# Expert tokens from a DRAM copy by indirect DMA in place of a one-hot gather on TensorE

## Chip, cores and metric

The kernel runs on one core of one Trainium2 chip. The metric is the device time of one launch in microseconds (us), the median of three runs. The profile is of one execution of the same program, taken by the hardware profiler.

## What is computed

Two layers of an encoder over 512 tokens of 1024 features (float32). Each layer has a mixer of two attention groups, a cross-attention into 256 memory tokens, and a mixture of experts. The last part is the one that matters here:

```python
def expert_choice_moe(h, w_router, w_gate, w_up, w_down):
    cap = EC_CAPACITY_FACTOR * S // N_EXPERTS            # 64 tokens for each of 16 experts
    affinity = jax.nn.softmax((h @ w_router).astype(jnp.float32), axis=-1)
    gate, idx = lax.top_k(jnp.swapaxes(affinity, 1, 2), cap)
    x_in = jax.vmap(lambda hb, ib: hb[ib])(h, idx)       # gather: (16, 64, 1024)
    a = jnp.einsum('becd,edf->becf', x_in, w_gate)       # w_gate, w_up: 1024 x 512 for each expert
    u = jnp.einsum('becd,edf->becf', x_in, w_up)
    y = jnp.einsum('becf,efd->becd', jax.nn.silu(a) * u, w_down)   # w_down: 512 x 1024
    y = y * gate[..., None]
    # y is added up at the tokens' places
```

h is the RMS-normalised x; the kernel gathers x itself and applies the gain and the token's inverse root afterwards. Every expert's weights are read once in a layer: 16 x 12 tiles of 512 KB.

## The kernel before

Everything up to the router works on x, which stays in SBUF, token-major in four blocks of 128 tokens. The rest of a layer, the expert stage, goes like this.

*Routing* (lines 912 to 984). `out_block` (865) adds the last residual to a block of x, `features` and `logits` (875, 887) make its router logits, `affinity` (900) the softmax. DVE then finds each expert's 64 best tokens in eight steps of maximum and replacement (967 to 970), makes a mask and its running sum (974, 975), TensorE (PE) turns both to the tokens' side (980), and `pos` (984) holds each token's slot in each expert, or 0. In layer 1 `warm` (961) issues products that nothing reads behind the last four of the eight steps, and in both layers behind the two turns; in layer 0 PE makes the next layer's memory keys meanwhile (956).

*Copies of x.* `xh` and `xl` (938 to 950) are x split in two float32r parts, by ACT and POOL.

*Gather* (1042 to 1067). The experts go in pairs, 64 slots on each half of the partitions, and two pairs make a group. For a group DVE compares `pos` with `iota` to get one-hot matrices `oh` (1046). PE multiplies `xh` and `xl` with them (1058, 1059), four token blocks each, which gives the group's tokens feature-major, 128 features at a time (`fill`, eight times a group). ACT scales them by the gain into `xg` (1062). `up_half` calls the first three fills of a group ahead of its first products and one before each later step of the first pair.

*A pair* (1159 to 1185). PE's program order for a pair: half of the gate products (`up_half`, 16 records on PE), the transposes of the previous pair's hidden layer (`hid_t`, 1104), the other half, the previous pair's down products (1117), the pair's gate values (`gates`, 1080), half of the up products, the previous pair's `scatter` (1131: products with the transposed selection matrix, which DVE adds to x at 1132), `selection` (1073), the other half. A bank of PSUM is evacuated by ACT and DVE as needed; the hidden layer is made by ACT (silu) and DVE.

*Weights.* `use` (986 to 997) lists the 192 tiles of a layer in the order of their use. A ring of tiles in three pools holds them; `EW_A` and `EW_B` are the numbers of two of the pools. Some tiles of the first round go into places that other tiles take up later (`once`, 1001). Loads go out on SP's queue in the order of use; a load waits until PE has used up the tile whose place it takes. The first 17 tiles of layer 0 and 24 of layer 1 (`early`) are loaded before the routing, the rest of the first round during it.

The order within an engine is made by the Tile framework from the program's order and readiness as it models it, so it can differ a little from the program text. The line that fills xg:

```python
nc.scalar.activation(e.xg[:, d, :], pg[:, i * P:i * P + P], AF.Copy, scale=gain(l, G_FFN, d))
```

Of the kernel before, what the change touches and what calls it, by code (L numbers as in the profile page):

```python
# [9 lines left out]
F32 = mybir.dt.float32  # L10
F32R = mybir.dt.float32r
AF = mybir.ActivationFunctionType
ALU = mybir.AluOpType
# [15 lines left out]
EW_B = 8  # L29
# [28 lines left out]
def kernel(ctx: ExitStack, tc: tile.TileContext, a: dict, out: bass.AP):  # L58
# [4 lines left out]
    ps = ctx.enter_context(tc.tile_pool(name="ps", bufs=8, space=PSUM))  # L63

# [9 lines left out]
    # ---------------------------------------------------------------- constants  # L74
# [28 lines left out]
    # ---------------------------------------------------------------- helpers  # L103
# [17 lines left out]
    class Weights:  # L121
        """weight chunks in the order of their use, loaded and split one ahead"""
# [29 lines left out]
    class Norm:  # L152
        """RMS over the features of a token-major tile, from the sums over its two halves"""
# [10 lines left out]
        def rstd(self, b):  # L164
            """mean square + eps -> v, its inverse root -> r"""
# [12 lines left out]
    def softmax_exp(pool, s, n, groups=1, scale=None):  # L178
        """exp of the rows of s (PSUM [P, groups*n]), scaled, less their maximum, and the row sums"""
# [24 lines left out]
    # ================================================================ layers  # L204
    for l in range(L):
# [18 lines left out]
        def gemm_tok(his, los, ks, n, post=()):  # L224
            """all token blocks x n columns; post[chunk, block]: work emitted behind that part"""
# [40 lines left out]
        # ---------------- mixer input projection  # L266
# [23 lines left out]
        def rope_tables():  # L290
            """rope tables with the q / k gains (and the q scale) folded in"""
# [24 lines left out]
        def rope_heads(pt, b, dst, nh, tab):  # L316
            """RMS-norm and rope of nh heads of 64 in PSUM -> dst, [P, nh, 64] each"""
# [59 lines left out]
        # ---------------- attention: units of one 128-query block of one head, heads in pairs  # L377
# [34 lines left out]
        class Group:  # L412
            """one head group's output: RMS norm over its 512 features, its half of w_o, residual"""
# [865 lines left out]
```

## Time and profile before

| | us |
|---|---|
| median of three runs | 1239.08 (1237.15 to 1239.32) |
| span of the profiled execution | 1236.1 |
| time of the profiled execution as a run | not listed apart |
| PE busy | 1196.0 |
| DVE, ACT, POOL busy | 621.5, 513.8, 199.1 |
| weight and other bytes moved | 247.97 MB, 201 GB/s over the span |

The span runs from the first to the last instruction in the profile; a run's time has some 3 us around it. The profile names engines PE (matrix products), PEld (weight loads of PE, beside it), DVE, ACT, POOL and SP; a q behind the name is the engine's instruction or DMA queue. A float32 product stands as two records. "L1098" is line 1098 of the kernel. Busy PE is not PE at its peak, since products are pipelined; idle time of an engine off the path costs nothing.

### The profile page before, as it was taken

The page shows a single profiled execution, that of the slowest core. Times are in us where ns is not written, and L with a number is a line of the kernel's source. Part 1 is how long each engine was busy: PE and PEld are TensorE (multiplying, and loading weights), DVE is VectorE, ACT ScalarE, POOL GpSimd, SP SyncE. Part 2 cuts the span into 40 slices and gives each one's busy share as a digit, 9 for nine tenths or more (in the row PEclk, how much of TensorE's full clock was granted, in tenths as well). Part 3 has the DMA queues.
Part 4 walks back from the last instruction along what each step waited for, and adds up shares of the span by engine and source line. Part 5 has one row for each costly group of instructions (what it writes and reads, how often), then busy time and mean ns, then how long its engine had stood idle before and what let it go on. Part 6 is the DMA issues. An engine that isn't in the chain of part 4 may idle for free.

```text
span 1236.1 us, 17348 instructions
## 1 busy us (share of the span) xinstructions
PE 1196.0 (97%) x6356; PEld 781.5 (63%) x6356; DVE 621.5 (50%) x1389; ACT 513.8 (42%) x1148; POOL 199.1 (16%) x234
## 2 busy tenths in 40 slices
PE   7999999999999999999999899999997999999995
PEld 7977777887773545443399677778864544443432
DVE  4898876556451222222377987755466032322124
ACT  5388766545432212120154886755553211110203
POOL 2533323100030000000124343230004000000002
PEclk9999999999999999999999999999997899999998
DMA  5410011493089999998124000128604599999942
GB/s 192 133 52 18 18 35 35 143 335 136 21 321 360 355 409 400 409 361 340 56 78 153 18 18 18 35 75 312 227 18 184 178 408 356 409 402 409 352 159 85
DMA packets 75621, 247.97 MB, mean 201 GB/s; under 512 B 8208, under 2 KB 18320, under 8 KB 75536
## 3 DMA queue, kind: packets, MB, share of 16 engines
q1 hardware_dynamic: 75104, 246.23, 52.9%
q8 instruction: 50, 0.82, 0.3%
q10 hardware_dynamic: 432, 0.63, 0.2%
q14 instruction: 35, 0.29, 0.1%
HBM read 244.73 MB, written 2.10 MB: 200 GB/s over the span
## 4 chain that ended last, share of the span: by engine, by line
PE 90%; DVE 5%; ACT 2%; issue 1%; POOL 1%; DMA 1%; SPq 0%; POOLq 0%; ACTq 0%; DVEq 0%
PE ps L1098 20%; PE ps L144 11%; PE ps L145 10%; PE ps L146 10%; PE ps L1117 9%; PE ps L1131 5%; PE ps L407 5%; PE ps L393 4%; PE ps L1058 3%; PE ps L1059 3%; DVE smm L181 2%; PE ps L488 1%; PE ps L804 1%; PE ps L847 1%; PE ps L250 1%
## 5 line engine op out<-in xcount | busy, mean ns | idle before, releaser
L1098 PE MATMUL ps<-ew,xg 128*64 128x512 f32 x1024 | 257.2, 602 | 0.0
L114 DVE TENSOR_TENSOR y<-ps,y 128x512 fp32r<-128x512 f32 x32 | 22.1, 692 | 234.0 <-ACT y L113 233.7
L1098 PEld LDWEIGHTS ps<-ew,xg 128*64 128x64 f32 x1024 | 69.0, 136 | 111.0 <-issue 96.7
L1117 PE MATMUL ps<-ew,hT 128*64 128x512 f32 x512 | 120.6, 594 | 0.0
L114 DVE TENSOR_TENSOR wlo<-raw,whi 128x1024 fp32r<-128x1024 f32 (+2 forms) x72 | 82.3, 1146 | 56.8 <-ACT whi L113 55.0
L181 DVE TENSOR_REDUCE smm<-ps 128x1 f32<-128x512 f32 (+1 forms) x144 | 97.7, 682 | 17.6 <-PE ps L488 7.0
L1132 DVE TENSOR_TENSOR x<-ps,x 128x512 f32<-128x512 f32 x128 | 80.0, 684 | 52.0 <-PE ps L1131 52.0
L187 ACT ACTIVATE P<-ps,smm 128x512 f32<-128x512 f32 x128 | 88.8, 697 | 27.9 <-DVE smm L181 22.3
L113 ACT CAST whi<-raw 128x1024 fp32r<-128x1024 f32 (+2 forms) x72 | 70.0, 974 | 65.6 <-PE ps L145 36.8
L196 POOL TENSOR_TENSOR P<-P,smr 128x512 f32<-128x512 f32 x64 | 70.4, 1100 | 155.8 <-DVE smr L194 127.0
L113 ACT CAST y<-ps 128x512 fp32r<-128x512 f32 x32 | 18.8, 587 | 157.8 <-PE ps L1117 138.5
L1117 PEld LDWEIGHTS ps<-ew,hT 128*64 128x64 f32 x512 | 37.6, 137 | 70.8 <-issue 67.5
L393 PE MATMUL ps<-ident,P 128*128 128x128 f32 x512 | 76.7, 273 | 4.0 <-POOL P L196 1.9
L1062 ACT ACTIVATE xg<-ps,gains 128x128 f32<-128x128 f32 x128 | 40.1, 364 | 95.1 <-PE ps L1059 94.9
L144 PE MATMUL ps<-whi,hTh 128*128 128x384 f32 (+2 forms) x224 | 79.0, 353 | 0.2 <-ACT whi L113 0.2
L145 PE MATMUL ps<-whi,hTl 128*128 128x384 f32 (+2 forms) x224 | 78.1, 348 | 0.0
L146 PE MATMUL ps<-wlo,hTh 128*128 128x384 f32 (+2 forms) x224 | 77.8, 350 | 0.0
L393 PEld LDWEIGHTS ps<-ident,P 128*128 128x128 f32 x512 | 62.1, 140 | 24.3 <-issue 3.9
L1131 PE MATMUL ps<-y,sel 128*128 128x512 f32 x256 | 69.1, 408 | 1.5 <-ACT y L113 1.5
L1131 PEld LDWEIGHTS ps<-y,sel 128*128 128x128 f32 x256 | 45.3, 188 | 38.5 <-issue 22.7
L1058 PEld LDWEIGHTS ps<-oh,xh 128*128 128x128 f32 x256 | 48.7, 191 | 32.7 <-issue 30.0
L1058 PE MATMUL ps<-oh,xh 128*128 128x256 f32 x256 | 68.2, 302 | 0.0
(224 smaller groups left out, 2272.6 us busy)
## 6 DMA issues: line engine op xcount, KB each, us to landing
ew<-moe SPq DMA_DIRECT2D x382, 512.0 KB, 8.6
raw<-w_o SPq DMA_DIRECT2D x16, 512.0 KB, 3.2
raw<-w_mem_v SPq DMA_DIRECT2D x8, 512.0 KB, 4.0
raw<-w_mem_q SPq DMA_DIRECT2D x8, 512.0 KB, 4.1
raw<-w_mem_o SPq DMA_DIRECT2D x8, 512.0 KB, 3.6
raw<-w_in_c SPq DMA_DIRECT2D x8, 416.0 KB, 3.7
raw<-w_in_a SPq DMA_DIRECT2D x8, 384.0 KB, 4.7
raw<-w_in_b SPq DMA_DIRECT2D x8, 384.0 KB, 3.8
```

What stands on the lines that cost most here:

```text
L113: i = nc.scalar.copy(dst_hi, src)
L114: nc.vector.tensor_tensor(out=dst_lo, in0=src, in1=dst_hi.bitcast(F32), op=ALU.subtract)
L144: nc.tensor.matmul(o, lh, rh, start=start, stop=False)
L145: nc.tensor.matmul(o, ll, rh, start=False, stop=False)
L146: nc.tensor.matmul(o, lh, rl, start=False, stop=stop)
L181: nc.vector.tensor_reduce(out=m, in_=s.rearrange("p (g n) -> p g n", g=groups), axis=AX.X, op=ALU.max, negate=True)
L187: nc.scalar.activation(p[:, g * n:(g + 1) * n], s[:, g * n:(g + 1) * n], AF.Exp, bias=m[:, g:g + 1], scale=1.0 if scale is None else scale ...
L393: nc.tensor.transpose(pt[:, tb * P:(tb + 1) * P], u.p[:, tb * P:(tb + 1) * P], ident)
L1058: nc.tensor.matmul(pg[:, :256], xh[:, b, d * P:(d + 1) * P], oh[:, b, :], start=b == 0, stop=False)
L1098: nc.tensor.matmul(acc[i * 64:i * 64 + 64, :], e.xg[:, k, i * 64:i * 64 + 64], ch[i][j % 2], start=k == 0, stop=k == 7)
L1117: nc.tensor.matmul(e.py[i * 64:i * 64 + 64, :], e.hT[:, f, i * 64:i * 64 + 64], ch[i][j], start=f == 0, stop=f == 3)
L1131: nc.tensor.matmul(o, sl, e.y[n][i], start=i == 0, stop=i == 1)
```

## The change

In each layer x's blocks are written to a DRAM tensor `xrows` as the router needs them. For each pair, four products of its one-hot matrix with the gate values, to which two columns of token numbers are added, give gates and token numbers together; DVE copies the numbers to integers, and POOL issues an indirect DMA that fetches the 128 rows of 1024 features. PE transposes them (`features_of`), and ACT fills xg with the gain as before. `xh`, `xl` and the gather products are gone. Pairs 0 and 1 are fetched at the start, pair p + 2 in the midst of pair p. The one-hot matrices have two buffers. `EW_B` goes from 8 to 12, and `once` loses its first two places. The `warm` products take x in float32, 256 columns, where they took xh with 512. The last block's output goes into ring tiles where it went into xh's place. Comments and docstrings are removed as well.

```diff
-EW_B = 8
+EW_B = 12
...
+    hbm = ctx.enter_context(tc.tile_pool(name="hbm", bufs=1, space=bass.MemoryType.DRAM))
...
+    ids = const.tile([P, NB], F32, name="ids")
...
+        nc.sync.dma_start(ids, a["ids"])
...
+        xrows = hbm.tile([S, D], F32, name=f"xrows{l}")
...
             if n == 1:
+                nc.scalar.dma_start(xrows[b * P:(b + 1) * P, :], x[:, b, :])
                 ffn_norm.rstd(b)
...
-        affs = mp.tile([P, NB, NE, 2, 2], F32R, name=nm("affs"))
+        affs = mp.tile([P, NB, NE // 2, 10], F32R, name=nm("affs"))
...
-        for b in range(NB):
-            nc.scalar.copy(xh[:, b, :], x[:, b, :])
-            nc.gpsimd.tensor_tensor(out=xl[:, b, :], in0=x[:, b, :], in1=xh[:, b, :].bitcast(F32), op=ALU.subtract)
...
+        for q in range(NE // 2):
+            nc.gpsimd.tensor_copy(affs[:, :, q, 8:10], ids.unsqueeze(2).broadcast_to([P, NB, 2]))
...
-        work = mp.tile([P, 2, S], F32, tag="oh", name=nm("work"), bufs=1)
+        work = mp.tile([P, 2, S], F32, tag="oh", name=nm("work"), bufs=2)
...
-                nc.tensor.matmul(idle, xh[:, 0, 0:P], xh[:, 0, 0:512], start=True, stop=True)
+                nc.tensor.matmul(idle[:, 0:256], x[:, 0, 0:P], x[:, 0, 0:256], start=True, stop=True)
...
-        once = {7: ((mp, "sg", 1), (mp, "sel", 1)), 21: (mp, "xg", 3), 22: (mp, "y", 2), 23: (mp, "y", 2)}
+        once = {22: (mp, "y", 2), 23: (mp, "y", 2)}
...
+        def features_of(e, n):
+            if n == 0:
                 e.xg = mp.tile([P, ND, P], F32, tag="xg", name=nm("xg"), bufs=3)
-
-            def fill(d):
-                pg = bank()
-                for b in range(NB):
-                    nc.tensor.matmul(pg[:, :256], xh[:, b, d * P:(d + 1) * P], oh[:, b, :], start=b == 0, stop=False)
-                    nc.tensor.matmul(pg[:, :256], xl[:, b, d * P:(d + 1) * P], oh[:, b, :], start=False,
-                                     stop=b == NB - 1)
-                for i, e in enumerate(prs):
-                    nc.scalar.activation(e.xg[:, d, :], pg[:, i * P:i * P + P], AF.Copy, scale=gain(l, G_FFN, d))
...
+            pt = bank()
+            for i in range(4):
+                d = n * 4 + i
+                nc.tensor.transpose(pt[:, i * P:(i + 1) * P], e.rows[:, d * P:(d + 1) * P], ident)
+            for i in range(4):
+                d = n * 4 + i
+                nc.scalar.activation(e.xg[:, d, :], pt[:, i * P:(i + 1) * P], AF.Copy, scale=gain(l, G_FFN, d))
...
-        def gates(e):
+        def fetch(e):
             pgt = bank()
             for b in range(NB):
-                nc.tensor.matmul(pgt[:, 0:8], e.oh[:, b, :],
-                                 affs[:, b, 2 * e.p:2 * e.p + 2].rearrange("p e h c -> p (e h c)"),
-                                 start=b == 0, stop=b == NB - 1)
-            e.gt = mp.tile([P, 2], F32, tag="gt", name=nm("gt"), bufs=2)
+                nc.tensor.matmul(pgt[:, 0:10], e.oh[:, b, :], affs[:, b, e.p, :], start=b == 0, stop=b == NB - 1)
+            at_row = mp.tile([P, 1], mybir.dt.int32, tag="row", name=nm("row"), bufs=4)
+            nc.vector.tensor_copy(at_row, pgt[:, 8:9])
+            e.rows = mp.tile([P, D], F32, tag="rows", name=nm("rows"), bufs=2)
+            nc.gpsimd.indirect_dma_start(out=e.rows, out_offset=None, in_=xrows,
+                                         in_offset=bass.IndirectOffsetOnAxis(ap=at_row, axis=0))
+            e.gt = mp.tile([P, 2], F32, tag="gt", name=nm("gt"), bufs=4)
...
+        one_hot(0)
+        for e in prs[:2]:
+            fetch(e)
+        for n in range(2):
+            features_of(prs[0], n)
+        for e in prs:
+            end = e.p == NE // 2 - 1
+            if e.p % 2 == 0 and not end and e.p + 2 < NE // 2:
+                one_hot(e.p // 2 + 1)
+            ag = bank()
+            up_half(e, ag, 0, 0)
+            if prev is not None:
+                hid_t(prev)
+            if not end:
+                features_of(prs[e.p + 1], 0)
+            up_half(e, ag, 0, 1)
...
+            up_half(e, au, 1, 0)
+            if not end:
+                features_of(prs[e.p + 1], 1)
+                if e.p + 2 < NE // 2:
+                    fetch(prs[e.p + 2])
+            if prev is not None and not end:
+                for n in range(2):
+                    scatter(prev, n)
+            if not end:
+                selection(e)
+            up_half(e, au, 1, 1)
```

## Rows read from the trace of the kernel before

**Rows 1.** The page, part 1: busy us, share of the span, instructions.

```profile
PE 1196.0 (97%) x6356; PEld 781.5 (63%) x6356; DVE 621.5 (50%) x1389; ACT 513.8 (42%) x1148; POOL 199.1 (16%) x234
```

**Rows 2.** Stretches: length, busy us of engines (x count), clock, DMA share, GB/s.

```profile
380.00:586.00 206.00, 205.90 (x1000) 93.05 (x1000) 50.27 (x94) 34.23 (x80) 0.00 (x0) 1.00 0.98 383
...
1020.00:1040.00 20.00, 20.00 (x108) 9.26 (x108) 1.09 (x4) 4.89 (x13) 0.00 (x0) 1.00 0.88 326
1040.00:1060.00 20.00, 20.00 (x98) 8.58 (x95) 6.56 (x12) 1.86 (x3) 0.00 (x0) 1.00 1.03 411
```

**Rows 3.** The chain that ended last, layer 1: start us, us, engine and line.

```profile
981.20 3.58 PE ps L1098 x16
...
992.27 0.59 PE ps L1104 x4
...
1043.10 3.86 PE ps L1131 x16
...
1209.31 0.66 PE ps L1104 x4
...
1220.66 1.89 PE ps L1117 x8
```

**Rows 4.** By line, 980 to 1180: busy us, mean ns, idle before, releasers.

```profile
L1098 PEld LDWEIGHTS ps<-ew,xg 128*64 128x64 f32 x412 | 27.2, 136 | 43.6 <-issue 37.1 <-DMA ew<-moe 2.4 <-ACT xg L1062 0.9
```

**Rows 5.** Weight loads of layer 1, then SP's waits (us in total, times, longest).

```profile
L1021 SPq DMA_DIRECT2D ew<-moe x156: 327/328/1177, 970.4 to 1182.0; - x156
...
DMA to landing us min/median/max: 3.6/9.2/11.0
...
SPq L1021 <- PE ps L1098: 94.0, 44, 18.3
```

**Rows 6.** Timeline near 1000 to 1034: start us, us, engine, line, idle before.

```profile
1003.24 0.61 PE L1080 MATMUL ps<-affs,oh 128*128 128x8 f32 x4
...
1003.88 0.15 DVE L1087 COPY g<-ps 64x2 f32<-64x2 f32 x1 [2.63 <-PE ps L1080]
...
1015.09 0.39 PE L1058 MATMUL ps<-oh,xh 128*128 128x256 f32 x1
...
1031.94 2.31 PE L1117 MATMUL ps<-ew,hT 128*64 128x512 f32 x10
```

**Rows 7.** Stretches of 2 us in layer 1, columns as in rows 2.

```profile
944.00:946.00 2.00, 0.01 (x1) 0.00 (x0) 1.88 (x4) 2.00 (x4) 1.85 (x5) 0.65 0.56 185
...
962.00:964.00 2.00, 2.00 (x7) 1.71 (x7) 1.43 (x4) 0.00 (x0) 0.00 (x0) 0.50 0.00 0
...
966.00:968.00 2.00, 2.00 (x14) 1.19 (x13) 0.00 (x0) 1.44 (x5) 0.00 (x0) 1.00 0.03 8
```

**Rows 8.** Timeline, start of the expert stage in layer 0.

```profile
343.73 12.25 PE L847 MATMUL ps<-ew,ew 128*128 128x256 f32 x56
...
358.51 1.44 DVE L1046 TENSOR_TENSOR oh<-pos,iota 128x256 fp32r<-128x256 f32 x4
...
359.12 0.28 PE L1058 MATMUL ps<-oh,xh 128*128 128x256 f32 x1
```

**Rows 9.** Timeline, start of the expert stage in layer 1.

```profile
951.28 1.65 PE L965 MATMUL ps<-xh 128*128 128x512 f32 x3
...
956.45 1.21 DVE L975 TENSOR_TENSOR_SCAN work<-ones,work 16x512 f32<-16x512 f32 x1
...
959.16 0.60 PE L980 MATMUL ps<-ident,work 16*128 16x16 f32 x4
...
962.10 1.43 DVE L1046 TENSOR_TENSOR oh<-pos,iota 128x256 fp32r<-128x256 f32 x4 [0.23 <-PE ps L963]
963.02 0.33 PEld L1058 LDWEIGHTS ps<-oh,xh 128*128 128x128 f32 x1
```

**Rows 10.** Small transfers: KB, median us to landing; then ns of an ACT issue.

```profile
out<-fo SPq DMA_DIRECT2D x4, 512.0 KB, 2.7
...
L1192 ACTq DMA_DIRECT2D lnf<-lnf x1: 334/334/334, 1212.2 to 1212.2; - x1
```

More of the change, by code (lines that the diff above doesn't have):

```diff
@@ L1039, with one_hot @@
         class Experts:
-        def gather(g):
-            oh = mp.tile([P, NB, 256], F32R, tag="oh", name=nm("oh"), bufs=1)
+            pass
+        prs = [Experts() for _ in range(NE // 2)]
+        ohs = {}
+        def one_hot(g):
+            oh = mp.tile([P, NB, 256], F32R, tag="oh", name=nm("oh"), bufs=2)
             for b0, nb in ([(b, 1) for b in range(NB)] if g == 0 else [(0, NB)]):
@@ L1094, in up_half @@
                     ch = [chunk(2 * e.p + i, w * 4 + k // 2) for i in range(2)]
-                while e.fill and len(e.fill) > ND - 3 - k:
-                    e.fill.pop(0)()
                 for i in range(2):
@@ L1134, in scatter @@
                     if b == 0:
-                        e.out = mp.tile([P, NB, D], F32, tag="xh", name=nm("fo"))
-                    nc.gpsimd.tensor_tensor(out=e.out[:, b, ns], in0=x[:, b, ns], in1=lnf[:, ns], op=ALU.mult)
+                        e.out = []
+                    pool, tag, bufs = ring[(len(use) + b - len(ring) - len(once)) % len(ring)]
+                    e.out.append(pool.tile([P, D], F32, tag=tag, name=nm("ew"), bufs=bufs))
+                    nc.gpsimd.tensor_tensor(out=e.out[b][:, ns], in0=x[:, b, ns], in1=lnf[:, ns], op=ALU.mult)
                 elif last:
@@ L1139, in scatter @@
                     last_norm.rstd(b)
-                    final(b, e.out[:, b, :])
+                    final(b, e.out[b])
         def half(b, n):
@@ L1158 @@
         prev = None
-        for g in range(4):
-            for e in gather(g):
-                ag = bank()
-                up_half(e, ag, 0, 0)
-                if prev is not None:
-                    hid_t(prev)
-                up_half(e, ag, 0, 1)
-                if prev is not None:
-                    for n in range(2):
-                        down(prev, n)
-                gates(e)
-                au = bank()
-                up_half(e, au, 1, 0)
-                end = e.p == NE // 2 - 1
-                if prev is not None and not end:
-                    for n in range(2):
-                        scatter(prev, n)
-                if not end:
-                    selection(e)
-                up_half(e, au, 1, 1)
-                if end:
-                    scatter(prev, 0)
-                sg = mp.tile([P, FF], F32, tag="sg", name=nm("sg"), bufs=1)
-                nc.scalar.activation(sg, ag, AF.Silu, scale=e.gt[:, 1:2])
-                nc.vector.scalar_tensor_tensor(out=sg, in0=au, scalar=e.gt[:, 0:1], in1=sg, op0=ALU.mult, op1=ALU.mult)
-                e.hid = sg
-                before, prev = prev, e
+        one_hot(0)
@@ new lines @@
+        for e in prs[:2]:
[13 more added lines that the diff above has]
+            up_half(e, ag, 0, 1)
+            if prev is not None:
+                for n in range(2):
+                    down(prev, n)
+            au = bank()
+            up_half(e, au, 1, 0)
[4 more added lines that the diff above has]
+            if prev is not None and not end:
+                for n in range(2):
+                    scatter(prev, n)
+            if not end:
+                selection(e)
+            up_half(e, au, 1, 1)
+            if end:
+                scatter(prev, 0)
+            sg = mp.tile([P, FF], F32, tag="sg", name=nm("sg"), bufs=1)
+            nc.scalar.activation(sg, ag, AF.Silu, scale=e.gt[:, 1:2])
+            nc.vector.scalar_tensor_tensor(out=sg, in0=au, scalar=e.gt[:, 0:1], in1=sg, op0=ALU.mult, op1=ALU.mult)
+            e.hid = sg
+            before, prev = prev, e
```

21 lines of the change are left out of this document (10 added, 11 removed).

## The prediction, made before the changed kernel was run

> **What bounds the kernel now.** I read the page first, then the busy time by stretch, then TensorE's own timeline, the chain that ended last, the waits on weights, the DMA queue, and the start of the expert stage in both layers. TensorE (PE) is busy 97% of the span [rows 1]. Each expert stage, about 359 to 620 us and 963 to 1236 us, is a stretch in which PE never rests (205.9 of 206 us) while the weight stream runs at 383 GB/s, and at 411 GB/s in its best 20 us [rows 2]. The reader is to see that two resources stand near their limits here, so that taking work from one pays only until the other binds.
>
> Which one binds now is read from three places. The chain that ended last goes through PE pieces almost alone in this stage [rows 3]. PE waited for weights 2.4 us in 200 [rows 4]. And the stream dips to 326 GB/s in a stretch in which PE makes gather products, since a weight tile is loaded only when PE has released one. So PE is the bound and the stream follows it; before the first release SP stands still 18.3 us [rows 5].
>
> **The gather products leave.** In layer 1 a whole group's gather lies between 1015.09 and 1031.94 us on PE, 16.85 us [rows 6]. In it stand two up halves at 3.58 us and one set of four transposes at 0.59 us [rows 3]. What is left, 16.85 - 7.16 - 0.59 = 9.1 us, is the 64 products and their changeovers. Four groups make 36.4 us in a layer. In layer 1 the first group's first two microseconds ran at a granted clock of 0.50 [rows 7], which is 1.0 us more: 37.4 us. All of it lies on the path. The 16 activations that fill xg for a group stay the same in number, so ACT gains nothing.
>
> **The transposes come.** Eight for a pair, in two sets of four like those of the hidden layer: 0.59 us a set [rows 3]. Sets of pairs 1 to 7: 14 x 0.59 = 8.3 us a layer, on the path. Pair 0's belong to the start, below.
>
> **The start of each stage.** Before, the first gather product follows the first of four one-hot blocks; layer 0: blocks from 358.51 to 359.95, product at 359.12 [rows 8]; layer 1: 962.10 to 963.53, PE at 963.02 [rows 9]. Afterwards PE can do nothing useful until x's rows are there. The steps: the last row-number product and its copy on DVE, about 0.65 us after the last block (four gate products started at 1003.24 had DVE start at 1003.88 [rows 6]); the indirect DMA, F; four transposes and the first activation, 1.1 us (0.59, and 0.5 estimated from that same hand-over). No indirect DMA, nor any DMA from POOL, stands in the trace. F is bounded below by the quickest 512 KB transfer, 2.7 us [rows 10], and above by the slowest weight landing, 11.0 us [rows 5]. Below zero is excluded, since nothing can start earlier. In layer 0 the weights are still streaming in at that moment, so I take 7; in layer 1 the queue is idle and I take 5, nearer the quiet row, with something for POOL's issue.
> First up product, layer 0: 359.95 + 0.65 + 7 + 1.1 = 368.7, that is 9.6 us after the old first gather product. Layer 1: 963.53 + 0.65 + 5 + 1.1 = 970.3, 7.3 us after.
>
> The clock: PE lost its full clock within two microseconds of falling idle (0.65 in 944 to 946 us) and worked at 0.50 still at 962 to 964 us [rows 7]. A wait of five microseconds or more will cost it again; it came back within some 3 us of dense work (1.00 at 966 to 968), so half speed costs 1.5 us, in each layer.
>
> Trainium skill, "DMA: Bandwidth & Descriptors", section on the GpSimd path: a DMA takes about 2.0 us plus its bytes over 436 GB/s. For 512 KB that would be 3.2 us; by it the whole sum below would be 5.6 us better. No run here shows it yet.
>
> **The warm-up products in layer 1** change from 512 columns of fp32r to 256 of fp32. An fp32 product of 256 columns takes 12.25/28 = 0.44 us at full clock [rows 8], so 0.88 at half; three make 2.6 us against 1.65 now [rows 9]. They already delay the routing: the mask is ready when the scan starts, 956.45, but PE turns it only at 959.16 [rows 9]. If the clock stays at half, four calls and the later single product make 4.3 us; if the denser products bring the clock up, the 2.7 us of delay could vanish instead. Between -2.7 and +4.3 I take +2, since the clock stayed at 0.50 throughout this pattern before.
>
> **Edits costed at little.** The four writes of x to DRAM go out on ACT's queue: 0.33 us of issue each [rows 10]. Three are hidden under a PE that is full there; the last stands before the copies that the last logits wait for: 0.3 us a layer. If an issue had to wait for a weight transfer ahead of it, ACT would be held for up to that transfer's 9.2 us, in layer 0 alone, where weights load at that moment; I keep that for the range. Their 2.1 MB are 5.1 us of transfers at 411 GB/s, before PE wants weights. The POOL subtractions and ACT casts of x lay beside DVE's top-k steps, which last until 956.45 [rows 9]: nothing gained. The eight index copies on POOL take their place under the same cover. The ids load is one more small DMA on SP at the start, behind work of PE. The tiles: 37 and 38 weights are loaded before PE starts, instead of 35 and 36 (four tiles more, two places of the first round fewer).
>
> **The fetches of later pairs** are issued one pair ahead. Between issue and use PE has a scatter 3.86, two up halves 7.16 and two sets of transposes 1.2: 12.2 us [rows 3]; less 1.7 for the hand-overs, F may be 10.5 without cost. I count nothing; pair 2 has no scatter before it, so some 3.9 us less cover. POOL, which waits for the row numbers, has nothing behind them in its queue until the last norm; DVE's copy of them waits for PE, and behind it stand the gate copies and the scatter's additions, on an engine busy for 50 of 206 us [rows 2].
>
> **Does the weight stream hold?** Before, 156 of a layer's 192 tiles were loaded after the start of layer 1 [rows 5]; with 38 ahead it is 154, and six fetches of the same size; at 0.524 MB over 411 GB/s [rows 2], 1.28 us each, 205 us. From about 972 us they are issued by 1177 and landed by 1186 (9.2 us [rows 5]). The last down products start at 1220.66 before [rows 3], so about 1202 afterwards: 16 us to spare.
>
> **Sum.** Layer 0: -36.4 + 8.3 + 9.6 + 1.5 + 0.3 = -16.7. Layer 1: -37.4 + 8.3 + 7.3 + 1.5 + 2 + 0.3 = -18.0. Together -34.7 on a span of 1236.1: 1201.4. The runs' median stands 3.0 us above that span, the profiled execution having no time of its own in the list: **1204 us**.
>
> **Rivals.**
> *The stream binds.* 221 us for 160 transfers (205 and the 16 to spare) are 380 GB/s; if the fetches, or two queues side by side, push it lower, PE waits at the end of each stage. Speaking for it: it already runs within 7% of its best on average [rows 2], and seven tiles are in flight at a time (9.2 us at 1.28). Against: the dips are PE's own. At 351 GB/s 160 transfers take 239 us, 18 too many in each layer, and nothing is left of the gain; midway, at 365, they take 230, 9 too many: 1222. At the dip's 326 it would be 257 and a loss. Chance 0.20, of which 0.05 at no change.
> The Trainium skill, same page, table of specifications, has about 358 GB/s as the HBM limit of one core: by it 160 transfers would take 234 us, and the time would be 1230. The trace does not agree: 411 GB/s [rows 2].
>
> *The rows come late for every pair.* PE takes its instructions in order; a transpose that waits for rows holds all up products behind it. Place: the first set of transposes of pairs 2 to 7, 12 in all. Price: 12 x (F - 10.5), and 2 x (F - 6) for the starts. It ends slower than before from F = 12.5 us on (24 + 13 = 37); at F = 14 it is 42 + 16 = 58, so 1262 us. For it: weight tiles take up to 11.0 us to land when the queue is full [rows 5], and no row shows what POOL needs to issue such a DMA. Against: a transfer on a queue of its own need not stand behind the seven weight tiles in flight. Chance 0.13.
>
> **Chances.** The forecast, 1193 to 1216 (both F at their ends give -6.6 to +10, the warm-up -4.7 to +2.3), 0.62; the stream 0.20; late rows 0.13; better than 1193, 0.05. What lies within 0.2%, some 2.5 us, a measurement of this kernel can't tell from no change. Faster: 0.62 + 0.15 + 0.05 = 0.82; same 0.05; slower 0.13. The range 1193 to 1232 holds the forecast and most of the first rival.
>
> **What would show it.** Right: the hidden layer's transposes, 31.0 us apart on average now (992.27 to 1209.31 for seven pairs [rows 3]), about 28.3 apart (less 27.3/7, plus 1.2); no gather lines; PE's first up product near 369 and 970 us; no wait of the transposes on the fetch beyond pair 0; the stream near 400 GB/s to the end. Wrong: PE waiting for weights by tens of microseconds late in a stage (first rival), or twelve waits on rows (second), or a first fetch of over 11 us.

## The result and the profile after

The changed kernel takes 1206.05 us (median of 4 runs, 1205.18 to 1207.55), the kernel before 1238.93 us (4 runs, 1237.15 to 1239.32): a ratio of 0.9738 with a 95% interval of 0.9724 to 0.9751. The forecast was 1204 us, faster. The profiled execution has a span of 1203.9 us and took 1205.65 us.

The page of the changed kernel: busy time and share of TensorE, its granted clock in 40 slices, and the chain that ended last, by engine and by line (up products are L1108 now, down products L1127, scatter products L1141, the transposes of fetched rows L1072).

```profile
PE 1146.7 (95%) x5992; PEld 741.2 (62%) x5992; DVE 622.8 (52%) x1405; ACT 500.5 (42%) x1140; POOL 197.6 (16%) x258
...
PEclk9999999999998999999999999999999799999998
...
PE 82%; DMA 7%; DVE 6%; ACT 2%; issue 1%; POOL 0%; SPq 0%; POOLq 0%; DVEq 0%; ACTq 0%
PE ps L1108 17%; PE ps L147 11%; PE ps L148 10%; PE ps L149 10%; PE ps L1127 8%; PE ps L1141 5%; PE ps L410 5%; DMA ew<-moe 4%; PE ps L396 4%; DMA rows<-xrows,row 2%; PE ps L1072 2%; DVE smm L184 2%; PE ps L491 2%; PE ps L807 1%; PE ps L253 1%
```

TensorE is busy for two points less of a shorter span [rows 1]. Two DMA entries stand in the chain, the fetch of the rows (2%) and the weights (4%). The first is the price that was forecast. Of the second some 36 us lie in layer 1, between 1118 and 1163 us, and point to something that was not.

By layer, between the same instructions of both kernels: from the last out-projection addition of layer 0 to the next layer's first transposes 620.27 - 337.55 = 282.7 us before and 607.02 - 337.33 = 269.7 after, so -13.0 (forecast -16.7); the mixer of layer 1 317.7 and 317.4; its expert stage to the end of the span 298.2 and 279.5, so -18.7 (forecast -18.0).

The start of the expert stage of layer 0 after the change, from the timeline (start, duration, engine, line, operation, count, and in brackets the idle time before it with what ended it), and of layer 1 behind the dots:

```profile
359.71 2.57 DVE L1056 TENSOR_TENSOR oh<-pos,iota 128x256 fp32r<-128x256 f32 x5
...
360.80 1.14 PE L1089 MATMUL ps<-affs,oh 128*128 128x10 f32 x8
362.19 0.15 DVE L1091 CAST row<-ps 128x1 int32<-128x1 f32 x1
...
363.21 1.21 POOL L1093 DMA_INDIRECT rows<-xrows,row  x1 [15.94 <-DMA ew<-moe]
...
370.90 1.94 PE L1072 MATMUL ps<-ident,rows 128*128 128x128 f32 x8 [8.97 <-DMA rows<-xrows,row]
...
372.77 4.82 PE L1108 MATMUL ps<-ew,xg 128*64 128x512 f32 x16
...
395.61 0.66 PE L1072 MATMUL ps<-ident,rows 128*128 128x128 f32 x4 [1.49 <-DMA rows<-xrows,row]
...
952.59 1.08 POOL L1093 DMA_INDIRECT rows<-xrows,row  x1 [18.87 <-DVE gt L1100]
...
957.05 1.94 PE L1072 MATMUL ps<-ident,rows 128*128 128x128 f32 x8 [5.62 <-DMA rows<-xrows,row]
...
958.92 5.29 PE L1108 MATMUL ps<-ew,xg 128*64 128x512 f32 x16
```

From POOL's issue to the first transpose the rows take 7.7 us in layer 0, beside a full weight stream, and 4.5 in layer 1, beside an idle one. TensorE stands idle 8.97 and 5.62 us and then starts at half clock: eight transposes take 1.94 us, and the first 16 up records 4.82 and 5.29 where 3.58 is usual [rows 3]. In front of the row number stands a one-hot block that nobody needs yet: the fifth of the five DVE instructions, 1.14 us, is that of the next group. Of the later fetches only pair 2's is waited for, 1.49 us here and 0.41 in layer 1. The clock, in stretches of 4 us (TensorE busy, granted clock, DMA share, GB/s):

```profile
362.00:366.00 4.00, 0.00 (x0) 0.87 1.03 421
366.00:370.00 4.00, 0.00 (x0) 0.50 1.02 413
370.00:374.00 4.00, 3.10 (x12) 0.50 0.54 213
```

TensorE's last product before them ended at 361.9 us; within the first of these stretches the clock fell to the lower of its two levels, 1.2 GHz.

### The profile page after: what moved, and what is told of

It is laid out like the page before. It is cut to its first block, busy times and chain, and to the rows that moved or that the text cites. A ratio compares the mean times of both kernels' runs of the same rounds, so it can differ in the third digit from the quotient of the medians.

```text
span 1203.9 us, 16694 instructions
## 1 busy us (share of the span) xinstructions
PE 1146.7 (95%) x5992; PEld 741.2 (62%) x5992; DVE 622.8 (52%) x1405; ACT 500.5 (42%) x1140; POOL 197.6 (16%) x258
## 4 chain that ended last, share of the span: by engine, by line
PE 82%; DMA 7%; DVE 6%; ACT 2%; issue 1%; POOL 0%; SPq 0%; POOLq 0%; DVEq 0%; ACTq 0%
PE ps L1108 17%; PE ps L147 11%; PE ps L148 10%; PE ps L149 10%; PE ps L1127 8%; PE ps L1141 5%; PE ps L410 5%; DMA ew<-moe 4%; PE ps L396 4%; DMA rows<-xrows,row 2%; PE ps L1072 2%; DVE smm L184 2%; PE ps L491 2%; PE ps L807 1%; PE ps L253 1%
## 5 line engine op out<-in xcount | busy, mean ns | idle before, releaser
L1108 PE MATMUL ps<-ew,xg 128*64 128x512 f32 x1024 | 256.6, 604 | 0.3 <-DMA ew<-moe 0.3
L1108 PEld LDWEIGHTS ps<-ew,xg 128*64 128x64 f32 x1024 | 74.6, 138 | 138.4 <-issue 121.6
L1127 PE MATMUL ps<-ew,hT 128*64 128x512 f32 x512 | 118.5, 594 | 0.2 <-DMA ew<-moe 0.2
L116 ACT CAST y<-ps 128x512 fp32r<-128x512 f32 x32 | 18.7, 585 | 157.0 <-PE ps L1127 154.2
L1127 PEld LDWEIGHTS ps<-ew,hT 128*64 128x64 f32 x512 | 38.0, 137 | 72.9 <-issue 70.0
L1141 PE MATMUL ps<-y,sel 128*128 128x512 f32 x256 | 70.3, 411 | 1.5 <-ACT y L116 1.5
L1093 POOL DMA_INDIRECT rows<-xrows,row x16 | 15.4, 962 | 332.0 <-DVE g L1099 296.5
L399 ACT COPY PT<-ps 128x512 f32<-128x512 f32 x96 | 56.0, 588 | 24.5 <-PE ps L396 24.0
L1141 PEld LDWEIGHTS ps<-y,sel 128*128 128x128 f32 x256 | 45.4, 188 | 31.6 <-issue 17.0
L1075 ACT ACTIVATE xg<-ps,gains 128x128 f32<-128x128 f32 x128 | 36.3, 372 | 67.7 <-PE ps L1072 67.7
```

The costliest lines, as they stand in the source:

```text
L116: i = nc.scalar.copy(dst_hi, src)
L1108: nc.tensor.matmul(acc[i * 64:i * 64 + 64, :], e.xg[:, k, i * 64:i * 64 + 64], ch[i][j % 2], start=k == 0, stop=k == 7)
L1127: nc.tensor.matmul(e.py[i * 64:i * 64 + 64, :], e.hT[:, f, i * 64:i * 64 + 64], ch[i][j], start=f == 0, stop=f == 3)
L1141: nc.tensor.matmul(o, sl, e.y[n][i], start=i == 0, stop=i == 1)
```

## The experiments

Two theories stood at first. **TensorE bounds the stage**: what the change took out of it (about 28 us in a layer) comes off the time, less the wait at the start. **The weight stream bounds it**, or rows are late: then work on TensorE is worth little. All twelve runs, with the kernel before on the same chip beside each:

| run | median us (range) | ratio to the kernel before, 95% interval |
|---|---|---|
| fixed rows at the start | 1191.3 (1190.8 to 1191.7) | 0.9621 (0.9605 to 0.9637) |
| half the weight bytes | 1169.3 (1167.8 to 1169.8) | 0.9440 (0.9424 to 0.9456) |
| before, gathered once | 1189.3 (1188.6 to 1189.3) | 0.9601 (0.9585 to 0.9618) |
| fetched twice | 1276.1 (1274.0 to 1277.2) | 1.0307 (1.0290 to 1.0324) |
| program order | 1185.2 (1185.0 to 1185.6) | 0.9580 (0.9550 to 0.9610) |
| program order, gains on POOL's queue | 1179.8 (1178.5 to 1181.5) | 0.9534 (0.9503 to 0.9564) |
| before, program order | 1214.9 (1211.7 to 1215.7) | 0.9823 (0.9792 to 0.9854) |
| eight tiles | 1204.8 (1203.3 to 1205.5) | 0.9741 (0.9710 to 0.9773) |
| idle products in the wait | 1177.3 (1176.3 to 1179.2) | 0.9519 (0.9502 to 0.9537) |
| and one-hots later | 1176.9 (1175.9 to 1178.1) | 0.9509 (0.9493 to 0.9525) |
| program order, gains, eight tiles | 1188.6 (1187.1 to 1189.0) | 0.9604 (0.9587 to 0.9621) |
| one-hots later, eight tiles | 1183.0 (1181.9 to 1185.8) | 0.9567 (0.9548 to 0.9586) |

**Fixed rows at the start.** Pairs 0 and 1 take their rows from token numbers that are known early; emitted before the top-k steps.

```diff
+        for i in range(2):
+            nc.vector.tensor_copy(at_row, ids[:, i:i + 1])
...
+            nc.gpsimd.indirect_dma_start(out=t, out_offset=None, in_=xrows,
+                                         in_offset=bass.IndirectOffsetOnAxis(ap=at_row, axis=0))
```

> The changed kernel, but pairs 0 and 1 of each layer get fixed token rows, fetched before the routing is known (the output is that of other tokens for these two pairs). Theory (the layer's start waits for the rows, and PE is otherwise the bound): the idle time of 8.97 and 5.62 us ahead of the first transposes goes, and so does what the low clock behind it cost (transposes 1.94 instead of about 1.3 us, the first 16 up products 4.75 and 5.22 instead of 3.58 us, together about 4 us): 1206 - 18.6 = 1187 us, 1184 to 1191. Rival (the weight stream sets the end of the stage, so an earlier start is given back as waits on weights): over 1200 us, with waits of PE on weights of ten us and more where there are 0.5 now.

Measured 1191.3, 14.7 us less than the changed kernel. The waits ahead of pair 0 are gone, and its up products run at full clock (this kernel's timeline):

```profile
362.56 3.65 PE L1119 MATMUL ps<-ew,xg 128*64 128x512 f32 x16
...
945.09 3.65 PE L1119 MATMUL ps<-ew,xg 128*64 128x512 f32 x16
```

So the waits and the half clock at the start are what was supposed. But 4 us of their price did not come off, and the time lies 0.3 us above the theory's range: in layer 0 the first pair's hidden transposes came 11.4 us earlier (382.09 for 393.46) and the last pair's only 7.7 (583.39 for 591.08), with 0.3 us of waits on weights in the records. Something later in the layer gives back; the distances below show where.

**Fetched twice.** Each fetch from pair 2 on is made a second time into the same tile.

```diff
-            nc.gpsimd.indirect_dma_start(out=e.rows, out_offset=None, in_=xrows,
+            for _ in range(2 if e.p > 1 else 1):
+                nc.gpsimd.indirect_dma_start(out=e.rows, out_offset=None, in_=xrows,
```

> The changed kernel, in which each fetch from pair 2 on is issued twice into the same tile; the second waits for the first to land, so the rows come after about 16.5 us instead of 8. Theory (a fetch is hidden as long as it is shorter than the stretch of PE work from its issue to its transposes, which the trace of the changed kernel shows as 7.5 us for pair 2, 11.1 us for pairs 3 to 5 and 14.0 us for pairs 6 and 7): PE waits 9.0, 3 times 5.4 and 2 times 2.5 us in a layer, against 1.49 and 0.41 us now, so about +57 us with both layers: 1263 us, 1245 to 1278, and slower than the kernel before. Rival (the transposes have far more slack than that, since other work runs ahead): within 10 us of 1206 us.

Measured 1276.1, at the top of the theory's range. TensorE's waits on rows in its list of waits (us in all, times, longest):

```profile
PE ps L1072 <- DMA rows<-xrows,row: 62.5, 13, 9.3
```

and three of them in the timeline of layer 0 (pairs 2, 3 and 6):

```profile
401.66 1.12 PE L1072 MATMUL ps<-ident,rows 128*128 128x128 f32 x4 [8.79 <-DMA rows<-xrows,row]
...
436.19 1.12 PE L1072 MATMUL ps<-ident,rows 128*128 128x128 f32 x4 [4.44 <-DMA rows<-xrows,row]
...
537.09 0.73 PE L1072 MATMUL ps<-ident,rows 128*128 128x128 f32 x3 [2.06 <-DMA rows<-xrows,row]
```

Expected were 9.0, 5.4 and 2.5. Of the 70 us the waits make 46.0 (62.5 for 16.5). The rest goes with a lower clock: the same 5992 TensorE instructions are busy 1169.0 us for 1146.7, at a mean granted clock of 0.96 for 0.985, and behind a wait of 4 us a set of transposes takes 1.12 us for 0.66. The rival of late rows was therefore real; the changed kernel is clear of it by 11.1 us of cover against landings of 7 to 9.

**Half the weight bytes.**

```diff
-                nc.sync.dma_start(t, src)
-                parts = [t[:, i * 512:i * 512 + 512] for i in range(2)]
+                nc.sync.dma_start(t[:, 0:512], src[:, 0:512])
+                parts = [t[:, 0:512] for i in range(2)]
```

> The changed kernel with only the first half of each expert weight tile loaded, and used for both halves (wrong weights, the same instructions on PE, half the bytes). Theory (PE bounds the expert stage, its waits on weights are 0.5 us in all): no gain from the weights themselves; only the fetches land sooner beside a thinner stream, which is worth at most the wait of pair 2 (1.49 and 0.41 us) and some 3 us at the start of layer 0 (landing 7.6 us there, 4.3 us in layer 1, where the queues were emptier): 1200 to 1206 us. Rival (the weight stream has become the bound of the stage): under 1190 us.

Measured 1169.3: 36.8 us less, where the first theory had at most 6. Read at face value, the stream is the bound. But TensorE had waited 0.5 us for weights in the changed kernel. What differs shows in the distance of one pair's hidden transposes to the next pair's, which I then read for every kernel (layer 0, us):

| kernel | pairs 0 to 7 |
|---|---|
| before | 33.4, 28.6, 33.4, 27.7, 38.3, 28.9, 26.8 |
| changed | 28.7, 27.0, 27.0, 27.3, 31.0, 30.5, 26.1 |
| fixed rows at the start | 28.5, 26.9, 27.3, 31.0, 31.0, 30.5, 26.1 |
| half the weight bytes | 27.0, 27.0, 27.0, 27.0, 27.0, 26.6, 19.9 |

The changed kernel runs at 27.0 and then loses 4.0, 3.9 and 6.2 us against half the bytes. With fixed rows one pair more is long (31.0 for 27.3): that is what was given back. In the changed kernel's timeline between 503.46 and 534.49 us TensorE is busy for 30.9 of 31.0 us (with some rows left out):

```profile
506.49 5.37 PE L1108 MATMUL ps<-ew,xg 128*64 128x512 f32 x24
511.69 7.04 PE L1127 MATMUL ps<-ew,hT 128*64 128x512 f32 x32
518.56 1.02 PE L1108 MATMUL ps<-ew,xg 128*64 128x512 f32 x2
...
520.37 0.48 PE L1141 MATMUL ps<-y,sel 128*128 128x512 f32 x1
520.78 1.93 PE L1108 MATMUL ps<-ew,xg 128*64 128x512 f32 x6
522.64 0.96 PE L1141 MATMUL ps<-y,sel 128*128 128x512 f32 x3
523.53 1.07 PE L1108 MATMUL ps<-ew,xg 128*64 128x512 f32 x2
524.53 0.96 PE L1141 MATMUL ps<-y,sel 128*128 128x512 f32 x3
525.43 1.93 PE L1108 MATMUL ps<-ew,xg 128*64 128x512 f32 x6
527.29 2.37 PE L1141 MATMUL ps<-y,sel 128*128 128x512 f32 x9
...
529.89 4.51 PE L1108 MATMUL ps<-ew,xg 128*64 128x512 f32 x18
```

and the same pair with half the bytes:

```profile
499.32 3.65 PE L1108 MATMUL ps<-ew,xg 128*64 128x512 f32 x16
502.80 7.04 PE L1127 MATMUL ps<-ew,hT 128*64 128x512 f32 x32
509.67 3.60 PE L1108 MATMUL ps<-ew,xg 128*64 128x512 f32 x16
...
514.06 3.98 PE L1141 MATMUL ps<-y,sel 128*128 128x512 f32 x16
...
518.26 7.09 PE L1108 MATMUL ps<-ew,xg 128*64 128x512 f32 x32
```

The same instructions stand in another order. An engine's order is fixed when the kernel is built, and the two kernels differ in their loads alone; that the build put scatter products and transposes ahead of up products whose weights it took to be late is inferred from this, not shown. The price is in the lengths: an up product has two records and runs beside its partner, which fills the other 64 columns. Runs of 16 and 32 records take 0.22 us a record. The runs of 2, 6 and 18 hold an odd number of products, so one is alone: a run of 2 takes 1.02 us and one of 6 takes 1.93, each some 0.6 us over that rate. Six of this pair's seven runs are odd, and its 64 up records take 17.8 us where a whole pair's take 14.3: 3.4 of the 4.0 us. Late weights are not in it, since TensorE's weight loads (PEld) wait for a weight tile at most 0.4 us there, where their usual step is 0.3. Still, this experiment changed two things, the bytes and the order, and can't say which was worth what. From the first to the last hidden transposes it takes 181.4 us in both layers, for 197.6 and 196.9; with 3.5 us less wait on rows at the starts (11.1 for 14.6, beside an emptier stream) that is 35.2 of its 36.8 us.

**Before, gathered once.** Groups 1 to 3 reuse the features of group 0.

```diff
-                e.xg = mp.tile([P, ND, P], F32, tag="xg", name=nm("xg"), bufs=3)
+                e.xg = mp.tile([P, ND, P], F32, tag="xg", name=nm("xg"), bufs=3) if g == 0 else xgs[i]
...
-            e.fill = [lambda d=d: fill(d) for d in range(ND)] if i == 0 else []
+            e.fill = [lambda d=d: fill(d) for d in range(ND)] if i == 0 and g == 0 else []
```

> The kernel before, with the gather products of the first group of experts alone; groups 1 to 3 reuse its gathered features (they compute on the wrong tokens). Theory (every PE instruction taken out of the stage shortens it): 3 groups of 9.1 us in 2 layers go, 1239 - 54.6 = 1184 us, 1182 to 1192. Rival (the weight stream was close behind PE, with some 16 us of slack in a layer): the slack caps the gain at about 32 us, 1207 us, with waits on weights that grow to make the difference.

Measured 1189.3, 49.1 us less than the kernel before, nearer the theory than the rival. Its pairs come every 26.3 us at first and every 29.3 from the fourth on, so here too late pairs give some back. With the turns of the kernel before in program order below (33.4 and 28.6, a mean of 31.0) a group's gather is 2 x (31.0 - 26.3) = 9.4 us.

**Program order.** To part order from bytes, each TensorE instruction of the stage is held behind the one written before it; in the changed kernel, in the kernel before, and with the load of the last norm's gains moved from ACT's queue to POOL's.

```diff
+        pin = tc.keep_in_program_order
...
-                    nc.tensor.matmul(acc[i * 64:i * 64 + 64, :], e.xg[:, k, i * 64:i * 64 + 64],
-                                     ch[i][j % 2], start=k == 0, stop=k == 7)
+                    pin(nc.tensor.matmul(acc[i * 64:i * 64 + 64, :], e.xg[:, k, i * 64:i * 64 + 64],
+                                     ch[i][j % 2], start=k == 0, stop=k == 7))
...
-            nc.scalar.dma_start(lnf, a["lnf"])
+            nc.gpsimd.dma_start(lnf, a["lnf"])
```

> The changed kernel with TensorE's instructions of the expert stage kept in the order of the program; nothing else is changed, all weights are loaded. In the changed kernel the pairs take 27.0 us each up to the fifth, and then 31.0, 30.5 and 26.1 us: there the order that the kernel was built with cuts the up products into runs of 1 to 12 with scatter products between them (64 up records take 17.8 us, 14.3 us before), and with half the weight bytes, where that order stays whole, the same pairs took 27.0, 26.5 and 19.9 us. Theory A (the cut order alone costs it, the weights are there): 14 us less in each layer, 1206 - 28 = 1178 us. Theory B (the weight stream sets the pace, 13.1 MB of a pair at 415 GB/s is 31.6 us, and the cut order only fills waits that come anyway): 1200 to 1210 us, with waits of PE on weights of 10 us and more in a layer. Between them, by the end of the stream (583 us in layer 0, ten us after the last up product would be done by A): some 1188 to 1195 us, with waits on weights at the ends of the layers alone.

> The kernel before with TensorE's instructions of the expert stage kept in the order of the program. Its pairs take 33.4 and 28.6 us by turns, but the fifth takes 38.3 us, and the last stretch 26.8 us. Theory A (cut order costs in the late pairs, less than in the changed kernel, as PE asked for weights more slowly): about 5 us of the fifth pair and up to 6 us of the last in each layer, 1239 - 10 to 22 = 1217 to 1229 us. Theory B (the stream sets the pace there): within 4 us of 1239 us. With the program-order kernel it gives what the change is worth when neither has a cut order: 36.4 - 8 - 10 us in layer 0 and 36.4 - 8 - 7 in layer 1 by the records, about 40 us in all, if PE is the bound in both.

> As the program-order kernel, and the load of the last norm's gains goes out on POOL's queue instead of ACT's. In the changed kernel SP's weight loads stood still for 19.5 us in layer 1 until that load had landed. Theory B or the case between (the stream paces the end of a layer): 5 to 9 us under the program-order kernel, all of it in layer 1. Theory A (the weights are there in time anyway): the same within 2 us. In both the standstill around 1100 us is gone from the rates.

Measured 1185.2, 1214.9 and 1179.8. The order alone is worth 20.9 us in the changed kernel and 22.6 in the one before: most of what theory A has, a little more than the case between, and for the kernel before just below the range. With both in program order the change is worth 1214.9 - 1185.2 = 29.7 us, and not the 40 that were expected if TensorE is the bound in both: the changed kernel's seven distances add up to 184.8 and 189.5 us, where half the bytes had 181.4. Distances in layer 0, and for the last kernel in layer 1:

| kernel | pairs 0 to 7 |
|---|---|
| before, program order | 33.4, 28.6, 33.4, 28.6, 33.4, 28.6, 20.6 |
| changed, program order | 28.4, 27.0, 27.0, 27.0, 27.0, 26.5, 21.8 |
| changed, program order, layer 1 | 27.0, 27.0, 27.0, 27.0, 27.0, 28.9, 25.6 |
| gains on POOL's queue, layer 1 | 27.3, 27.0, 27.0, 27.0, 27.0, 26.6, 23.2 |

What is left over the 19.9 us of half the bytes is the stream's. It hardly shows as idle time of TensorE's products. Busy time of the up products in the last two distances of layer 0, in program order (stretch, its length, PE and weight-load busy, clock, DMA share, GB/s):

```profile
530.13:556.67 26.54, 14.34 (x66) 4.42 (x64) 1.00 1.03 415
556.67:578.48 21.81, 12.46 (x50) 4.05 (x48) 1.00 1.03 412
```

and with half the bytes:

```profile
525.28:551.83 26.55, 14.35 (x66) 4.42 (x64) 1.00 0.65 209
551.83:571.71 19.88, 10.76 (x50) 3.36 (x48) 1.00 0.02 7
```

The same 50 records of the same order are busy 1.7 us longer where the stream is full. The transfers beside them do not lengthen them: in the stretch before, 66 records take 14.34 and 14.35 us beside 415 and 209 GB/s. What lengthens them are waits on weights, hidden in the busy time of products that run side by side; the weight loads (PEld) name them. Their waits in the program-order kernel (us in all, times, longest):

```profile
PEld ps L1110 <- DMA ew<-moe: 16.2, 38, 1.1
```

With half the bytes that row has 2.3 us, and no wait in it is longer than the usual step of 0.3. In the last distance of layer 0 four such waits make 2.5 us in program order, and with half the bytes there is none.

Layer 1 lost more, since SP's loads stood still, 11.9 us in program order and 19.5 in the changed kernel. There, SP's longest wait around 1100 us (us in all, times, longest):

```profile
SPq L1028 <- DMA lnf<-lnf: 19.5, 1, 19.5
```

the DMA issues of SP and ACT in its timeline:

```profile
1096.52 24.45 SPq L1028 DMA_DIRECT2D ew<-moe  x9
1114.20 0.34 ACTq L1215 DMA_DIRECT2D lnf<-lnf  x1
1117.68 2.31 SPq L1028 DMA_DIRECT2D ew<-moe  x5
```

the row of its 20 us with TensorE's busy time first and GB/s last:

```profile
1100.00:1120.00 20.00, 19.90 (x87) 8.48 (x85) 7.80 (x16) 3.96 (x9) 0.94 (x1) 1.00 0.48 164
```

and the same 20 us with the gains on POOL's queue:

```profile
1100.00:1120.00 20.00, 20.00 (x98) 7.36 (x95) 2.13 (x3) 3.59 (x9) 0.00 (x0) 1.00 1.03 410
```

A weight load on SP waited 19.5 us for a load of another engine's queue that had not even been issued, and that, by the program, for a buffer of one-hot matrices. The kernel before has no such wait: with one buffer for them its load of the gains went out at 1212.2 us [rows 10], behind the last weight load at 1182.0 [rows 5]. So it is the change's second buffer that lets the load into the weight stream. Moving the load was worth 5.4 us, with the last distances of layer 1 at 26.6 and 23.2 instead of 28.9 and 25.6. What it costs with the built order was not run; there the last two distances are 31.2 and 27.2 us in layer 1 for 30.5 and 26.1 in layer 0.

**The four tiles.**

```diff
-EW_B = 12
+EW_B = 8
```

> The changed kernel with eight weight tiles in the stage's own pool instead of twelve. In layer 0 the loads stop with all tiles full from 368 to 376 us, just ahead of the first up product, so four tiles less are 2.1 MB less ahead of PE, 5 us of the stream at 415 GB/s. Theory A (PE bounds, the weights are early): within 2 us of 1206 us, unless the built order is cut earlier. Theory B (the stream sets the pace of the late pairs): 5 us more in each layer, about 1216 us.

> The kernel of program order with the gains on POOL's queue (1179.8 us), with eight weight tiles in the stage's pool instead of twelve. With the built order these four tiles were worth nothing (1204.8 against 1206.1 us): the first rows of layer 0 landed earlier without them, beside an emptier stream, and the stage started some 4 us earlier there. Theory B (with the order kept the stream is only 3.4 us from the pace, so 2.1 MB less ahead of PE, 5 us at 415 GB/s, show at the end of the layers): 4 to 5 us earlier at the start of layer 0 and 5 us later at the end of it, 2 to 5 us later in layer 1: 1181 to 1186 us. Theory A (PE bounds it still): 1175 us.

With the built order eight tiles take 1204.8 us, twelve 1206.1: no difference that these runs show. In layer 0 the first fetch lands after 4.5 us for 7.6, beside a stream that has come to rest (18 GB/s from 360 to 364 us), and the first hidden transposes come 4.5 us earlier (388.94 for 393.46); the seven distances add up to 197.7 and 198.4 us for 197.6 and 196.9. With the order kept they take 1188.6 against 1179.8, 8.8 us more and beyond the 6 that were expected: the last distances in layer 0 grow from 26.5 and 22.4 to 27.6 and 25.8. Here read-ahead is worth nothing until TensorE asks fast enough.

**The start, on top of program order and moved gains.**

```diff
+        for _ in range((14, 8)[l]):
+            pin(nc.tensor.matmul(idle[:, 0:256], x[:, 0, 0:P], x[:, 0, 0:256], start=True, stop=True))
...
-                one_hot(e.p // 2 + 1)
+                with tc.issue_after(prs[e.p + 1].cast.ins):
+                    one_hot(e.p // 2 + 1)
```

> The kernel of program order with the gains on POOL's queue (1179.8 us), and 14 (layer 0) or 8 (layer 1) idle products of 256 columns on TensorE between the first row products and the first transposes, some 7.3 and 4.2 us of work inside waits of 8.3 and 5.6 us. Theory (the wait also lets the clock fall to half, and that costs: transposes 1.94 instead of 1.32 us, the first 16 up records 5.0 and 4.2 instead of 3.6 us): about 3 us less, 1177 us, 1174 to 1178, with the clock at 1.00 in the first up products. Rival (the clock falls whatever PE does there, or the stream of weights takes the gain back at the layer's end): within 1 us of 1179.8 us.

> As the kernel with idle products in the wait, and the one-hot matrices of the second group of experts, which stood ahead of the first row number on the vector engine (1.14 us), come behind it. Theory (the start of a layer is the chain row number, fetch, rows): 1.1 us less in each layer, about 2 us under the kernel with idle products. Rival (POOL's fetch waits for later instructions of that engine anyway, or the end of the layer is the stream's): within 0.7 us of it.

> As the kernel with idle products and the later one-hot matrices, with eight tiles instead of twelve, and 9 idle products in layer 0 instead of 14, for its shorter wait. Against that kernel the four tiles do what they do without the idle products: by theory B 1 to 6 us more, by theory A some 4 us less.

The idle products alone: 1177.3, 2.4 us less, in a range that touches the other kernel's; the mechanism shows in layer 1, where transposes and up products ran at full clock, while in layer 0 the 14 products were over in 6.3 us, and in a wait of 3.41 us the clock went again (granted 0.72 from 370 to 372 us and 0.50 in the next two):

```profile
371.15 1.94 PE L1074 MATMUL ps<-ident,rows 128*128 128x128 f32 x8 [3.41 <-DMA rows<-xrows,row]
373.02 4.26 PE L1110 MATMUL ps<-ew,xg 128*64 128x512 f32 x16
...
944.69 1.06 PE L1074 MATMUL ps<-ident,rows 128*128 128x128 f32 x8 [2.12 <-DMA rows<-xrows,row]
945.78 3.65 PE L1110 MATMUL ps<-ew,xg 128*64 128x512 f32 x16
```

The later one-hots: 1176.9, no difference shown; POOL's issue came 0.6 us earlier behind the row product in both layers, where 1.1 was expected. With eight tiles, and nine idle products in layer 0, the same kernel takes 1183.0, 6.2 us more, just above theory B's 1 to 6. The best of these kernels, at 0.951 of the time before, takes 29 us off the changed one, 26.3 of it by two edits: the order, which has nothing to do with the gather, and the gains' queue, whose trouble the change had brought in.

## Why the prediction was right, point by point

**The bound.** TensorE bounds the stage in the kernel before: shown. In program order its turns of 33.4 and 28.6 us hold to the end, and without three gathers it is 49 us faster. The change is worth 29.7 us when both kernels keep the program's order and 32.9 when neither does. The intervals of the two program-order kernels are some 4 us wide to either side, so these runs show no part of the gain that is the order's.

**The gather**, -36.4 us a layer: measured 9.4 us a group, -37.6. **The transposes**, +8.3: too much. In program order a pair takes 27.0 us, and 26.3 in the kernel before where it gathers nothing: 0.7 us a pair, 7 x 0.7 = 4.9. The step took 0.59 us for each set, the length of its records; from its start to the next product's a set costs 0.4 to 0.5, and the row product took the place of the gate product.

**The start**, +9.6 and +7.3, with +0.3 in both layers for the writes to DRAM and +2 in layer 1 for the warm-up products. Layer 0 took 21.6 us from its last out-projection addition to the first gather product (359.12 [rows 8]) and takes 35.4 to the first up product (372.77): +13.9 where 9.9 was forecast. In layer 1 (the addition at 937.94 before, 924.43 after) 25.1 us became 34.5: +9.4 where 9.6 was forecast, but by luck, as its parts show.

From the first one-hot block to the first up product the chain was 2.9 and 1.5 us longer than the step had it. F, taken as 7 and 5, was 7.6 and 4.3. The missing items were the one-hot block ahead of the row number (0.6, as in the run with the later one-hots), POOL's start (0.8 to 0.9 behind the row number), and the first transposes at half clock (1.9 us for 1.1).

The first top-k step came later in both layers, by 1.4 and 1.1 us from the same addition (in layer 0 at 345.15 us, before at 343.93), where 0.3 was priced for an issue on ACT's queue; the cause stays open. The warm-up products were priced at +2, because the clock had stayed at 0.50 throughout. It did not stay there (timeline, and stretches of 2 us, of the changed kernel):

```profile
942.03 1.56 PE L972 MATMUL ps<-x 128*128 128x256 f32 x6
...
938.00:940.00 2.00, 1.67 (x5) 1.07 (x6) 1.90 (x6) 0.00 (x0) 0.00 (x0) 0.50 1.04 418
942.00:944.00 2.00, 2.00 (x10) 1.31 (x10) 1.87 (x5) 0.00 (x0) 0.00 (x0) 1.00 1.03 420
```

From the mask's scan to the first one-hot block layer 1 took 5.7 us before (956.45 to 962.10 [rows 9]) and 5.2 after (944.01 to 949.20): -0.5.

By the Trainium skill, "DMA: Bandwidth & Descriptors", section on the GpSimd path, 512 KB would take 3.2 us, an estimate; no fetch in the trace was that quick (4.3 to 9.0 us, median 7.5). **The clock** behind it, +1.5: 1.2 and 1.7 us on the first up products.

**Fetches hidden**: right but for pair 2 (1.49 and 0.41 us), which the step had named as short of 3.9 us of cover and then costed at nothing. The threshold, F of 10.5 us, is borne out by the cover of 11.1 us in the trace and by the double fetch.

**The pace**: 28.3 us was forecast between hidden transposes; 197.6 / 7 = 28.2 was measured. It is right as a mean, by luck, and wrong as a picture: 28.7 with pair 2's wait in it, 27.0, 27.0 and 27.3, then 31.0, 30.5 and 26.1. The step took one mean (31.0) of a stage that already held a fifth pair of 38.3 us. Transposes at half the price gained 3 us a layer, and the late pairs lost about 3 us more than before: by the distances (4.0 + 3.9 + 6.2) - (4.9 + 0.3 + 6.2 - 0.9) = 3.6 us.

**The stream's 16 us to spare** held for a mean pace of 28 us: 0.5 us of waits of PE, and four tiles that are worth nothing. In program order it does not hold; there TensorE is through earlier and the last pairs wait. The rival's rate was wrong: with the fetches beside it the stream ran at 408 to 420 GB/s in every 10 us from 390 to 580 us. The Trainium skill, "DMA: Bandwidth & Descriptors", table of specifications, has about 358 GB/s as the HBM limit of one core; the trace, with this one core at work, does not agree.

**Sum.** With the measured terms layer 0 would have -37.6 + 4.9 + 13.9 + 1.2 + 1.5 + 3.6 = -12.5 (the result is -13.0), layer 1 -37.6 - 1.0 (the half clock of the old gather's start) + 4.9 + 9.4 + 1.7 + 0.4 + 4.3 = -17.9 (-18.7), where 4.3 is what its last four distances lost: 115.3 us for 100.4, less 121.7 for 111.1 before. So the mechanism held, and some of the closeness is luck. The start was undersized by 4 us in layer 0 and hit in layer 1 by a warm-up that went the other way; the transposes were oversized by 3 in each layer, and the late pairs, at nothing in the sum, lost about 4. The span was forecast at 1201.4 us and is 1203.9. The time came nearer than that, since a run stands 1.8 us above its span (1205.65 for 1203.9) and not the 3.0 that were added.

## What to carry to other kernels

Before costing a change, read the period of the repeated unit one by one, not as a mean: a unit that is longer without any idle time is an order of instructions or a hidden wait, and may hold more than the change. Keep the order of the engine that bounds when the build is free to rearrange it; here that is worth 21 us. Count with a fetch whose address is computed at the last moment for its whole chain (number, issue, landing, and the clock lost meanwhile), and put its landing beside the cover of each place where it is used.

## What the runs showed of the hardware that I had not expected

Products on 64 columns run beside their partner; one left alone by the order costs some 0.6 us. In the kernel of eight tiles in program order the records of products name twelve waits on weights of up to 0.2 us each, 2.3 us in all, while its last distance was 25.8 us instead of 19.9; the records of weight loads name 50 of up to 1.1 us, 25.7 us in all. A load on SP's queue waited 19.5 us for one on ACT's queue with which it shares no data, and no longer did when that went to POOL's; why the two were tied was not tried further. An indirect DMA of 128 rows holds POOL for 0.94 us (the first of a layer 1.1 to 1.2).
